# DRAM scratch of the attention operands in another axis order, and head outputs stored through another DMA queue

## The chip, the cores and the metric

The kernel runs on one core of a Trainium2 chip. The metric is the device time of one execution in microseconds (us). The kernel before takes 3268.81 us, the median of three runs (3268.14 to 3269.44).

## The reference

The program computes two layers of a transformer-like backbone on 512 latent and 256 context tokens (768 together) of width 1024. Each layer is a half-weight SwiGLU FFN, a token mixer and a second half-weight FFN, all with modulation, pre- and post-norm. The mixer of layer 0, which most of the change is about, is differential attention with 8 heads; each head has two score maps (m = 0, 1) over 64 features and one value matrix of 128 columns. Cut to what matters:

```python
q, k, v = split(h @ w_qkv)            # q, k: (n, 8 heads, 2 maps, 64); v: (n, 8, 128)
q_l, k_l = apply_rope(q_l), apply_rope(k_l)            # latent tokens only
s = einsum('bqhmd,bkhmd->bhmqk', q, k) * 64 ** -0.5
p = softmax(s, axis=-1)
a = p[:, :, 0] - lam * p[:, :, 1]
o = einsum('bhqk,bkhe->bqhe', a, v)
y = (rmsnorm(o, subln) * (1 - lam_init)) @ w_o
```

Context queries attend to context keys alone. The mixer of layer 1 is a bidirectional gated linear recurrence with 8 heads, whose normed and gated head outputs also go through an output projection.

## The kernel before

**Exact parts.** TensorE works on float32 numbers split in a high and a low part, hi + lo, each exact in its one-pass format (`split`, L187 on ScalarE and L188 on VectorE). A product is three matmuls: high times high, high times low, low times high.

**Attention by head pairs.** Layer 0's attention runs over four pairs of heads, p = 0 to 3. In a stage, TensorE projects the queries and then the keys of pair p (`proj`, L574) and its values (L1146), and between these matmuls it steps through the attention of pair p - 1 (`attn`); a `Ticker` deals out the steps in proportion to the TensorE work recorded. The projected q or k is rotated on GpSimd (`rotate`, L1120 to L1122), split into the tile `qkhl`, and stored to a DRAM scratch `st_d[p, w]` in one DMA of 128 partitions (`stored`, L1111). `qkhl` holds on its partitions (head and map j = 0 to 3, index i = 0 to 31) and along them (part v, rotation half a, token).

**Stacked operands.** The scores want the features of one head and map on 64 partitions, with both exact parts stacked to 128. `load_stack` (L896 to L914) reads the scratch back into such a tile `stk` (128 partitions, 5 columns of 768 tokens), one tile per head, in nine DMAs on the SP queue, all at L904: one of 128 rows and eight of 64 rows, each row 768 x 4 bytes. The scratch has the axes (v, a, j, i, token), so that the 64 rows of one part and one j are two runs of 32 rows that lie apart in DRAM. The stack of a pair's first head is asked for right behind the store of the keys, that of the second at the beginning of `attn`. The scores (L950, L951) then read `stk`; their row maximum is taken on VectorE (L953), the exponential on ScalarE (L960), the difference of the two maps on VectorE (L973), and its transposes on TensorE (L988) are split into `aT` (L990, L995) for the product with the values (L1008).

**Head outputs.** `finish` norms a head's values (L1029 on GpSimd, L1033 on TensorE, L1036 on VectorE) and stores them to DRAM, `on_d`, by one DMA on the SP queue (L1039). Layer 1 does the same at L1349. The output projection loads them again through the same ring of three buffers (`raw`, L158) through which all weights come: first `on_d`, then its part of the weights `da_wo`, head after head. While the last pair's attention runs, TensorE does the output projection of the first five heads (L653); the last three are left for `mixer_tail`.

**What sets the order.** Each engine runs its instructions in the order in which they were recorded. All loads and the stores named here are issued by SP one after the other, so that a DMA that waits holds back those behind it. A load into a `raw` buffer waits until the buffer's last user, a `split`, is done on VectorE (L188).

Of the kernel before, what the change touches and what calls it, by code (L numbers as in the profile page):

```python
# [23 lines left out]
NLAT = 512  # L24
# [16 lines left out]
def kernel(  # L41
# [56 lines left out]
    def ps_gv(shape):  # L98
# [6 lines left out]
        (p, w): dram.tile([2, 2, 4, 32, NTOK], F32, name=f"st_d{p}{w}") for p in range(NPAIR) for w in "qk"  # L105
# [24 lines left out]
    class Jobs:  # L130
        """Weight stream: loads run ahead of their use in the order of use."""
# [39 lines left out]
        def look(self, key, ahead):  # L171
            """Split up to the `ahead`-th unit after job key."""
            j = bisect.bisect_right(self.units, self.pos[key]) + ahead - 1
            self.upto(self.units[min(j, len(self.units) - 1)] + 1)

        def need(self, key, ahead=0):
            """The result of job key; the next `ahead` units are split beforehand too."""
            self.upto(self.pos[key] + 1)
            if ahead:
                self.look(key, ahead)  # L180
            return self.res.pop(key)
# [3 lines left out]
    def split(dst_hi, dst_lo, src):  # L185
        """src = dst_hi + dst_lo, both exact in the tensor engine's one-pass format."""
        nc.scalar.copy(out=dst_hi, in_=src)  # L187
        nc.vector.tensor_tensor(out=dst_lo, in0=src, in1=dst_hi.bitcast(F32), op=ALU.subtract)  # L188
# [21 lines left out]
    class Mods:  # L210
        """Modulation vectors: silu(c) w_mod + b_mod.  At the start, when the tensor engine is idle, on it, one
        contraction chunk per step; later the vector engine multiplies and adds up the contraction chunks, half of
        the columns at a time, and the tensor engine only sums over the partitions."""
# [11 lines left out]
        def start(self, parts, rings, wide=None):  # L225
            """wide: silu(c) padded to 32 columns, for the tensor engine."""
# [30 lines left out]
        def run(self):  # L257
            """On the tensor engine: one contraction chunk of one part per step."""
# [16 lines left out]
        def chunks(self):  # L275
            """On the vector engine: two contraction chunks of half of the columns per step."""
# [28 lines left out]
        def total(self, acc, l, part, h, nm):  # L305
            """Sums over the partitions."""
# [49 lines left out]
        def gains(self, g, si):  # L356
            """Post-norm gains times gates, as rows."""
# [6 lines left out]
        def pace(self, slots):  # L364
            """The vector engine's share of one of `slots` remaining places."""
# [6 lines left out]
        def due(self):  # L372
            """What is due on the tensor engine."""
# [29 lines left out]
    class Ticker:  # L403
        """Steps a generator of interleaved work in proportion to the tensor-engine time emitted."""
# [8 lines left out]
        def later(self, delay, fn):  # L413
            """fn after `delay` more of tensor-engine time."""
# [21 lines left out]
    class Events:  # L436
        """Calls at given places of the interleaved work."""
# [10 lines left out]
    class Boundary:  # L448
        """Post-norm, residual and the next pre-norm of one sub-layer, one token tile at a time."""
# [35 lines left out]
        def tail(self, emit_tile, extra={}):  # L485
            """emit_tile over the tiles; the norm stages of the tiles before it come at places of their own in each."""
# [38 lines left out]
        def advance(self, n):  # L525
            """The first n units of the feature-major modulated input of the next sub-layer, in two exact parts;
            a unit is two feature chunks of a block of 256 tokens."""
# [25 lines left out]
        def stream(self, mm):  # L553
            """mm(b, ks) over token blocks and pairs of feature chunks, behind the transposes."""
# [16 lines left out]
    def mm_k(ps_ap, w, mv, k, nk=KC):  # L571
        """One contraction chunk: the three products of the two exact parts of each side."""
# [5 lines left out]
    def proj(w, hT, pt, a, b, tick=None):  # L578
        """pt[:, :b-a] = w^T hT[.., a:b] over all of the contraction."""
# [27 lines left out]
    def add_o(l, tag, wsrc):  # L607
        """Heads below TAIL pass through the unit ring while the mixer's last heads are still computed."""
# [34 lines left out]
    def out_tile(t, aT, wos, y, firstg, tick=None, small=False):  # L643
        """Partial output projection of token tile t, added into y."""
# [27 lines left out]
    def ffn(l, i, fp, xt, B0, nt, nxt, mods, last=False, spill=False):  # L672
        """In- and out-projections in groups of d_ff chunks; returns the boundary to the next sub-layer."""
# [99 lines left out]
    with ExitStack() as st:  # L773
# [10 lines left out]
        # modulation vectors of the first pre-norm, through slots that the first FFN needs later  # L784
# [19 lines left out]
        # q of the first head pair, token block by token block as they become ready  # L804
# [51 lines left out]
    with ExitStack() as st:  # L856
# [23 lines left out]
        # lower bounds of the recurrence: softmax over depth, cumulative, less the first  # L880
# [15 lines left out]
        def load_stack(p, hh):  # L896
            """Scores' operands of one head: both exact parts stacked along the contraction.
            0, 1: queries of m = 0 (high, low) and m = 1 (low, high); 2, 3: the high part of the keys twice;
            4: the low part of the keys of both m."""
# [3 lines left out]
            def ld(p0, n, c, src):  # L903
                nc.sync.dma_start(out=st_[p0:p0 + n, c].bitcast(F32), in_=src)  # L904

            j = 2 * hh
            ld(0, 128, 0, q[:, :, j].rearrange("v a i t -> (v a) i t"))
            for m in range(2):
                for dup in range(2):
                    ld(64 * dup, 64, 2 + m, k[0, :, j + m])  # L910
                ld(64 * m, 64, 4, k[1, :, j + m])
            for v in range(2):
                ld(64 - 64 * v, 64, 1, q[v, :, j + 1])
# [14 lines left out]
        def attn(p, vh):  # L928
            """Attention of the two heads of pair p; yields between tensor-engine steps."""
# [36 lines left out]
            def combine(hh, t):  # L966
                """p0 - lam (s0 / s1) p1: s0 times the difference of the two softmaxes."""
# [33 lines left out]
            def av(hh, b):  # L1001
                """Values of one block of 256 queries."""
# [12 lines left out]
            def finish(hh):  # L1015
                """Norm of a head over its 128 values, gain, and store; the values are s0 times those of the softmax."""
# [22 lines left out]
                nc.sync.dma_start(out=on_d[0][2 * p + hh], in_=of)  # L1039
# [30 lines left out]
        def need_spread(key, ahead):  # L1070
            """As J.need, the units after it split while this one is used."""
# [14 lines left out]
        for p in range(NPAIR):  # L1086
            T.every = 45.5 / 42
            for wi, w in enumerate("qk"):
# [20 lines left out]
                def stored(ab_t=ab_t, hl=hl, w=w, p=p):  # L1109
                    split(hl[:, 0, :, NLAT:], hl[:, 1, :, NLAT:], ab_t[:, :, NLAT:])  # L1110
                    nc.sync.dma_start(out=st_d[p, w].rearrange("v a j i t -> (j i) (v a) t"),  # L1111
                                      in_=hl.rearrange("p v a t -> p (v a) t").bitcast(F32))
# [3 lines left out]
                def rotate(ab, ab_t=ab_t):  # L1116
                    """(A C - B S, A S + B C)"""
# [50 lines left out]
    def mixer_tail(l, tag, si, nt, nxt, fp, xp, outs):  # L1168
        """Last heads of the output projection and the boundary to the next FFN."""
# [18 lines left out]
    with ExitStack() as st:  # L1188
# [7 lines left out]
        # values of the first head pair, token block by token block  # L1196
# [15 lines left out]
    y_st = ExitStack()  # L1212
    with ExitStack() as st:
# [6 lines left out]
        def blk(ap, L):  # L1220
            """(blocks of 2L, halves, L) view of a token axis."""
            return ap.rearrange("p (n two l) -> p n two l", two=2, l=L)

        def scan(h, F, Kt, qv, gs, v2):
            """Both directions of head h.  F: decays; Kt: keys, then keys times the decays to the end of their
            block; qv: queries; Qt: queries times the decays from the start of their block; gs: silu(gate)."""
# [20 lines left out]
            def muls(lev):  # L1247
                """Queries and keys times the decays over the other half of the blocks of this level."""
# [238 lines left out]
```

## Time and profile before

| | |
|---|---|
| median of three runs | 3268.81 us |
| span of the profiled execution | 3260.0 us (no other time of that execution is given; the median is 8.8 us above it) |
| TensorE matmul busy | 3049.1 us (94%), 17,122 matmuls |
| VectorE, ScalarE, GpSimd busy | 1717.6, 962.2, 177.9 us |
| DMA moved | 321.76 MB, mean 99 GB/s |
| chain that ended last | TensorE 82%, DMA 4%, ScalarE 4%, VectorE 4%, SP's issue 3% |
| layer 0's attention in the span | from about 640 to 1210 us |

TensorE is busy nearly all the time, so what counts is where it is not, and what it was waiting for; a busy share of another engine says little by itself. A wait is put down to what came last. The column PEclk of the tables by stretch is the granted clock of TensorE as a share of full speed: 1.00 is 2.4 GHz, 0.50 is 1.2 GHz. The column "DMA share" is the mean busy share of the 16 DMA engines.

### The profile page before, as it was taken

What the parts mean: (1) busy time and instruction counts of PE and PEld (TensorE: products, weight loads), DVE (VectorE), ACT (ScalarE), POOL (GpSimd) and SP (SyncE); (2) the same over time, 40 slices, a digit from 0 to 9 for tenths busy, and PEclk for the clock granted to TensorE, in tenths of its full rate; (3) what the DMA queues carried; (4) which work ended last, traced back from release to release, by engine and by line L of the source; (5) the groups of instructions that cost most, each with busy time, mean ns of one, the idle gap of its engine ahead of it and who ended that gap; (6) DMA issues with size and microseconds to landing.
All of it is one profiled execution on the core that took longest, in us unless ns stands there. A gap on an engine that the chain in (4) does not pass through costs nothing.

```text
span 3260.0 us, 41074 instructions
## 1 busy us (share of the span) xinstructions
PE 3049.1 (94%) x17122; PEld 2577.9 (79%) x17122; DVE 1717.6 (53%) x2393; ACT 962.2 (30%) x1597; POOL 177.9 (5%) x219
## 2 busy tenths in 40 slices
PE   7999999967968589999999999999999999889998
PEld 5888888856757378888888888888889889678887
DVE  4556555634635367454444755444465666663344
ACT  4111111523424235111112411111263434442222
POOL 0000000311101001000000100000010000010000
PEclk9999999988989699999999999999999999999999
DMA  5333333222222232333322333333221111242221
GB/s 216 121 111 126 119 118 103 107 90 94 80 86 83 78 110 102 100 98 104 103 84 78 104 104 126 115 115 113 89 77 56 49 63 49 84 146 80 98 99 70
DMA packets 109066, 321.76 MB, mean 99 GB/s; under 512 B 10224, under 2 KB 10704, under 8 KB 108880
## 3 DMA queue, kind: packets, MB, share of 16 engines
q1 hardware_dynamic: 105232, 306.50, 27.8%
q0 software_dynamic: 1920, 6.34, 0.6%
q10 hardware_dynamic: 1728, 6.29, 0.5%
q8 instruction: 135, 2.21, 0.3%
q14 instruction: 51, 0.42, 0.0%
HBM read 292.83 MB, written 26.26 MB: 98 GB/s over the span
## 4 chain that ended last, share of the span: by engine, by line
PE 82%; DMA 4%; ACT 4%; DVE 4%; SPq 3%; issue 3%; POOL 1%; ACTq 0%; DVEq 0%; POOLq 0%
PE mm L574 41%; PE mm L653 20%; PE tp L574 9%; SPq L904 3%; PE tp L1370 2%; PE mm L1280 1%; PE tp L653 1%; PE mm L950 1%; PE gv L1008 1%; ACT tmp L395 1%; ACT tmp L545 1%; PE mm L951 1%; DMA mw<-in_w_mod_dram 1%; DMA stk<-st_d2q 1%; DMA stk<-st_d1q 1%
## 5 line engine op out<-in xcount | busy, mean ns | idle before, releaser
L574 PE MATMUL mm<-hT,hl 128*128 128x256 f32 (+1 forms) x7728 | 1407.6, 341 | 8.3 <-DVE hT L550 3.2
L574 PEld LDWEIGHTS mm<-hT,hl 128*128 128x128 f32 x7728 | 1199.3, 188 | 208.4 <-DVE hT L550 7.1
L653 PE MATMUL mm<-wo,a 128*128 128x512 f32 x2886 | 664.9, 390 | 0.5 <-DVE wo L188 0.5
L653 PEld LDWEIGHTS mm<-wo,a 128*128 128x128 f32 x2886 | 538.6, 188 | 115.4 <-DVE y L668 2.8
L670 DVE TENSOR_TENSOR y<-y,mm 128x1024 f32<-128x1024 f32 x163 | 199.0, 1221 | 500.0 <-PE mm L653 500.0
L188 DVE TENSOR_TENSOR hl<-raw,hl 128x1024 fp32r<-128x1024 f32 x250 | 306.8, 1238 | 173.2 <-ACT hl L187 173.1
L574 PE MATMUL tp<-hT,hl 128*128 128x512 f32 (+1 forms) x1824 | 381.8, 360 | 7.9 <-DVE aT L995 7.2
L574 PEld LDWEIGHTS tp<-hT,hl 128*128 128x128 f32 x1824 | 291.8, 192 | 53.8 <-DVE aT L995 9.3
L292 DVE SCALAR_TENSOR_TENSOR acc<-mw,cs,acc 128x512 f32<-128x512 f32 x392 | 271.5, 746 | 2.3 <-DMA mw<-in_w_mod_dram 0.7
L187 ACT CAST hl<-raw 128x1024 fp32r<-128x1024 f32 x250 | 258.2, 1046 | 47.2 <-DMA raw<-in_da_wo_dram 23.4
L187 ACT CAST a<-tmp 128x768 fp32r<-128x768 f32 (+1 forms) x88 | 68.8, 781 | 664.0 <-DVE tmp L747 664.0
L187 ACT CAST wo<-raw 128x1024 fp32r<-128x1024 f32 x94 | 98.1, 1045 | 462.6 <-PE mm L653 457.6
L731 ACT ACTIVATE tmp<-mm 128x768 f32<-128x768 f32 (+1 forms) x88 | 66.8, 759 | 406.7 <-PE mm L574 405.5
L747 DVE TENSOR_TENSOR tmp<-tmp,mm 128x768 f32<-128x768 f32 (+1 forms) x88 | 78.0, 886 | 201.1 <-PE mm L574 199.0
L950 PE MATMUL mm<-stk 128*128 128x512 f32 (+1 forms) x128 | 65.5, 511 | 97.6 <-DMA stk<-st_d3q 19.8
L953 DVE TENSOR_REDUCE nm<-mm 128x1 f32<-128x768 f32 (+1 forms) x96 | 73.3, 776 | 146.4 <-PE mm L951 143.6
L653 PE MATMUL tp<-hl,hT 128*128 128x512 f32 x300 | 92.0, 442 | 38.4 <-DVE aT L995 28.5
L950 PEld LDWEIGHTS mm<-stk 128*128 128x128 f32 (+1 forms) x128 | 25.4, 199 | 126.7 <-issue 112.0
L188 DVE TENSOR_TENSOR a<-tmp,a 128x768 fp32r<-128x768 f32 (+1 forms) x88 | 78.5, 892 | 74.6 <-ACT a L187 74.6
L188 DVE TENSOR_TENSOR wo<-raw,wo 128x1024 fp32r<-128x1024 f32 x94 | 114.8, 1223 | 5.5 <-ACT wo L187 5.5
L960 ACT ACTIVATE pt<-mm,nm 128x768 f32<-128x768 f32 (+1 forms) x96 | 72.7, 768 | 121.6 <-DVE nm L953 121.6
L653 PEld LDWEIGHTS tp<-hl,hT 128*128 128x128 f32 x300 | 57.6, 207 | 53.5 <-DVE aT L995 31.0
(187 smaller groups left out, 2448.8 us busy)
## 6 DMA issues: line engine op xcount, KB each, us to landing
raw<-in_w_in_dram SPq DMA_DIRECT2D x176, 512.0 KB
mw<-in_w_mod_dram SPq DMA_DIRECT2D x144, 512.0 KB
raw<-in_w_out_dram SPq DMA_DIRECT2D x88, 512.0 KB
raw<-in_hg_w_dram SPq DMA_DIRECT2D x32, 512.0 KB
raw<-in_da_qk_dram SPq DMA_DIRECT2D x16, 512.0 KB
gg<-gg_d POOLq DMA_DIRECT2D x12, 512.0 KB, 4.8
xp<-x_d SPq DMA_DIRECT2D x10, 512.0 KB
raw<-in_da_v_dram SPq DMA_DIRECT2D x8, 512.0 KB
```

Source lines behind the costliest of these rows:

```text
L187: nc.scalar.copy(out=dst_hi, in_=src)
L188: nc.vector.tensor_tensor(out=dst_lo, in0=src, in1=dst_hi.bitcast(F32), op=ALU.subtract)
L292: nc.vector.scalar_tensor_tensor(out=acc[:, m], in0=raw[:, kk], scalar=cs[:, k, m:m + 1], in1=acc[:, m], op0=ALU.mult, op1=ALU.add)
L574: nc.tensor.matmul(out=ps_ap, lhsT=w[a], rhs=mv[b], start=(k == 0 and i == 0), stop=(k == nk - 1 and i == 2))
L653: nc.tensor.matmul(out=po if small else po[:, hh * 512:(hh + 1) * 512], lhsT=aT[ci][:, u, t * P:(t + 1) * P], rhs=wos[ci][:, v, hh * 512:( ...
L670: nc.vector.tensor_tensor(out=dst, in0=dst, in1=src, op=ALU.add)
L731: nc.scalar.activation(out=sg[:, :width], in_=pg[:, :width], func=AF.Silu)
L747: nc.vector.tensor_tensor(out=sg[:, :width], in0=sg[:, :width], in1=pu[:, :width], op=ALU.mult)
L904: nc.sync.dma_start(out=st_[p0:p0 + n, c].bitcast(F32), in_=src)
L950: nc.tensor.matmul(out=sc[:, 0:NLAT], lhsT=lhs, rhs=rhs[:, 0:NLAT], start=(i == 0), stop=(i == 1))
L953: nc.vector.tensor_reduce(out=nm, in_=sc[:, :n], axis=AX.X, op=ALU.max, negate=True)
L960: nc.scalar.activation(out=pt[:, :n], in_=scs[m][:, :n], func=AF.Exp, bias=nms[m], accum_out=s0s[hh][:, t:t + 1] if m == 0 else s1)
```

## The change

The scratch `st_d` has the axes (j, v, a, i, token) in place of (v, a, j, i, token), so that the 64 rows of one part and one j lie one behind the other. The store of q or k is four DMAs of 32 partitions in place of one of 128. The stack of a head comes in ten loads of 64 consecutive rows, in place of one of 128 and eight of 64, and the operands of m = 0 come ahead of those of m = 1. The stores of head outputs, in both layers, are issued by GpSimd. The texts that describe functions are taken out, which changes no instruction but moves the line numbers: L904 becomes L905, L1111 L1116, L1039 L1043, L1349 L1354.

```diff
     st_d = {
-        (p, w): dram.tile([2, 2, 4, 32, NTOK], F32, name=f"st_d{p}{w}") for p in range(NPAIR) for w in "qk"
+        (p, w): dram.tile([4, 2, 2, 32, NTOK], F32, name=f"st_d{p}{w}") for p in range(NPAIR) for w in "qk"
     }
...
             q, k = st_d[p, "q"], st_d[p, "k"]
 
-            def ld(p0, n, c, src):
-                nc.sync.dma_start(out=st_[p0:p0 + n, c].bitcast(F32), in_=src)
+            def ld(half, c, src):
+
+                nc.sync.dma_start(out=st_[64 * half:64 * half + 64, c].bitcast(F32),
+                                  in_=src.rearrange("a i t -> (a i) t"))
 
             j = 2 * hh
-            ld(0, 128, 0, q[:, :, j].rearrange("v a i t -> (v a) i t"))
+            for v in range(2):
+                ld(v, 0, q[j, v])
             for m in range(2):
                 for dup in range(2):
-                    ld(64 * dup, 64, 2 + m, k[0, :, j + m])
-                ld(64 * m, 64, 4, k[1, :, j + m])
-            for v in range(2):
-                ld(64 - 64 * v, 64, 1, q[v, :, j + 1])
+                    ld(dup, 2 + m, k[j + m, 0])
+                ld(m, 4, k[j + m, 1])
+                if m == 0:
+                    for v in range(2):
+                        ld(1 - v, 1, q[j + 1, v])
             stk[p, hh] = st_
...
-                nc.sync.dma_start(out=on_d[0][2 * p + hh], in_=of)
+                nc.gpsimd.dma_start(out=on_d[0][2 * p + hh], in_=of)
...
-                    nc.sync.dma_start(out=st_d[p, w].rearrange("v a j i t -> (j i) (v a) t"),
-                                      in_=hl.rearrange("p v a t -> p (v a) t").bitcast(F32))
+                    for j in range(4):
+                        nc.sync.dma_start(out=st_d[p, w][j].rearrange("v a i t -> i (v a) t"),
+                                          in_=hl[32 * j:32 * j + 32].rearrange("p v a t -> p (v a) t").bitcast(F32))
...
-            nc.sync.dma_start(out=on_d[1][h][:, 0:NLAT], in_=of)
+            nc.gpsimd.dma_start(out=on_d[1][h][:, 0:NLAT], in_=of)
```

On SP, this is the order around the store of the keys of pair 2 in the kernel before (`st_d2k` is the scratch of pair 2's keys, `stk` a head's stack, `on_d_2` the output of head 2, `raw` a buffer of the weight stream):

```order
L1111 DMA st_d2k<-qkhl 128x4x768
L904 DMA stk<-st_d2q 128x1x768
L904 DMA stk<-st_d2k 64x1x768 x6
L904 DMA stk<-st_d2q 64x1x768 x2
L1039 DMA on_d_2_89<-of 128x768
L904 DMA stk<-st_d2q 128x1x768
L904 DMA stk<-st_d2k 64x1x768 x6
L904 DMA stk<-st_d2q 64x1x768 x2
L158 DMA raw<-in_da_v_dram 128x1024 x2
```

And this is the same place in the changed kernel:

```order
L1116 DMA st_d2k<-qkhl 32x4x768 x4
L905 DMA stk<-st_d2q 64x768 x2
L905 DMA stk<-st_d2k 64x768 x3
L905 DMA stk<-st_d2q 64x768 x2
L905 DMA stk<-st_d2k 64x768 x3
L905 DMA stk<-st_d2q 64x768 x2
L905 DMA stk<-st_d2k 64x768 x3
L905 DMA stk<-st_d2q 64x768 x2
L905 DMA stk<-st_d2k 64x768 x3
L158 DMA raw<-in_da_v_dram 128x1024 x2
```

The store of head 2's output has left SP; the two stacks follow each other, and one column of q (m = 1) has moved ahead of the second group of k.

On GpSimd, this is the order before around the norm factor `r` of the heads 0 and 1 and the first rotation of pair 2's q (`t`):

```order
L1029 TENSOR_TENSOR r_5768<-r_5768,halfc 128x6
L1029 TENSOR_TENSOR r_6174<-r_6174,halfc 128x6
L1120 TENSOR_TENSOR t_6515<-ab_t,CSt 128x512
L1121 TENSOR_TENSOR t_6516<-ab_t,CSt 128x512
L1122 TENSOR_TENSOR t_6515<-t_6515,t_6516 128x512
```

And this is that place in the changed kernel:

```order
L1033 TENSOR_TENSOR r_5779<-r_5779,halfc 128x6
L1043 DMA on_d_0_87<-of 128x768
L1033 TENSOR_TENSOR r_6189<-r_6189,halfc 128x6
L1043 DMA on_d_1_88<-of 128x768
L1125 TENSOR_TENSOR t_6531<-ab_t,CSt 128x512
L1126 TENSOR_TENSOR t_6532<-ab_t,CSt 128x512
L1127 TENSOR_TENSOR t_6531<-t_6531,t_6532 128x512
```

The stores of the heads 0 and 1 now stand on GpSimd, that of head 1 ahead of the rotation. The order on TensorE, VectorE and ScalarE is the same in both kernels.

## Rows read from the trace of the kernel before

**Rows 1.** TensorE's waits over the span: total us, times, longest us

```profile
PE tp L653 <- DVE aT L995: 28.5, 5, 25.9
```

**Rows 2.** Line 904: durations ns min/median/max; then who waited, us and times

```profile
L904 SPq DMA_DIRECT2D stk<-st_d1k x12: 484/3660/4187, 780.4 to 825.7; - x12
...
L904 SPq DMA_DIRECT2D stk<-st_d0q x6: 671/3698/3701, 659.2 to 715.6; - x6
...
  PE mm L950: 97.5, 11
```

**Rows 3.** Chain that ended last, 900 to 950 us: start, us, what

```profile
905.98 6.18 DMA st_d2k<-qkhl
...
928.73 19.64 DMA stk<-st_d2q
...
948.46 0.77 PE mm L950
```

**Rows 4.** Busy time by stretch; last columns PEclk, DMA share, GB/s

```profile
684.00:688.00 4.00, 0.00 (x0) 0.00 (x0) 0.00 (x0) 0.00 (x0) 0.00 (x0) 0.50 0.13 51
...
1188.00:1192.00 4.00, 4.00 (x28) 3.52 (x26) 1.20 (x3) 2.57 (x4) 0.00 (x0) 1.00 0.83 317
```

**Rows 5.** SP and TensorE in order of time, where the pairs' scores begin

```profile
658.60 0.38 SPq L1111 DMA_DIRECT2D st_d0k<-qkhl  x1
...
774.17 0.38 SPq L1111 DMA_DIRECT2D st_d1k<-qkhl  x1
...
1029.91 0.37 SPq L1111 DMA_DIRECT2D st_d3k<-qkhl  x1
...
676.77 0.77 PE L950 MATMUL mm<-stk 128*128 128x512 f32 x1 [4.97 <-DMA stk<-st_d0k]
...
793.33 0.47 PE L950 MATMUL mm<-stk 128*128 128x512 f32 x1 [0.28 <-DMA stk<-st_d1k]
...
924.39 0.47 PE L950 MATMUL mm<-stk 128*128 128x512 f32 x1 [3.62 <-DMA stk<-st_d2k]
...
1047.82 0.50 PE L653 MATMUL tp<-hl,hT 128*128 128x512 f32 x1 [3.00 <-ACT hl L187]
1048.39 0.60 PE L950 MATMUL mm<-stk 128*128 128x512 f32 x1
```

**Rows 6.** ScalarE, SP and VectorE in order of time, last pair

```profile
1115.08 1.04 ACT L187 CAST hl<-raw 128x1024 fp32r<-128x1024 f32 x1 [23.43 <-DMA raw<-in_da_wo_dram]
...
1096.64 3.61 SPq L158 DMA_DIRECT2D raw<-in_da_wo_dram  x1
...
1079.80 0.96 DVE L188 TENSOR_TENSOR hT<-raw,hT 128x768 fp32r<-128x768 f32 x1
```

**Rows 7.** Busy time of nine stretches behind TensorE's waits, the longest and their sum

```profile
1073.00:1089.00 16.00, 16.00 (x46) 11.74 (x47) 7.72 (x12) 7.21 (x14) 1.99 (x1) 0.50 0.13 50
...
sum 57.00, PE 44.00 PEld 31.74 DVE 22.80 ACT 15.99 POOL 4.00; mean PE 4.89 PEld 3.53 DVE 2.53 ACT 1.78 POOL 0.44
```

**Rows 8.** GpSimd's loads of gains (count, busy us, mean ns; then us to landing)

```profile
L386 POOL DMA_DIRECT2D gg<-gg_d x12 | 6.8, 567 | 685.9 <-DMA raw<-in_w_in_dram 460.6 <-DVE acc L292 225.2
...
DMA to landing us min/median/max: 3.8/4.8/5.4
```

**Rows 9.** SP and VectorE in order of time, end of attention; GpSimd and ScalarE, a rotation

```profile
1199.46 0.33 SPq L1039 DMA_DIRECT2D on_d<-of  x1
...
1203.29 3.49 DVE L188 TENSOR_TENSOR wo<-raw,wo 128x1024 fp32r<-128x1024 f32 x3
...
831.71 2.01 POOL L1120 TENSOR_TENSOR t<-ab_t,CSt 128x512 f32<-128x512 f32 x1 [5.63 <-ACT ab_t L1103]
...
849.83 0.47 DVE L1036 SCALAR_TENSOR_TENSOR of<-of,sub,gv 128x256 f32<-128x256 f32 x1
...
857.88 0.63 ACT L187 CAST qkhl<-t 128x512 fp32r<-128x512 f32 x1
```

**Rows 10.** TensorE's waits from 1700 us to the end, the longest

```profile
PE tp L541 <- ACT y L483: 7.9, 4, 4.4
```

## Prediction

> **What bounds the kernel now.** I read TensorE's waits first, since TensorE is busy 94% of the span. Nearly all that it waits for is in layer 0's attention: 97.5 us in 11 pieces of the scores (L950) for the stacked operands [rows 2], and 25.9 us in one piece of the output projection (L653) that is put down to VectorE [rows 1]. From 1700 us on no wait for a DMA is among TensorE's; the longest there, 7.9 us, is for ScalarE [rows 10]. So the change can gain in the attention and hardly elsewhere.
>
> The chain of waits says how a stage begins: the keys' store takes 6.2 us, then SP issues loads, and the last of these, q of m = 1, is what the scores wait 19.6 us for [rows 3]. The loads are slow one by one. A load of 64 rows (196,608 B) holds SP for 3.70 us and one of 128 rows (393,216 B) for 3.70 us as well [rows 2]. While they run the 16 DMA engines are busy to a share of 0.13, that is 2 of 16, at 51 GB/s; with all engines in use 317 GB/s go through at a share of 0.83 [rows 4]. A 64-row load has two runs of rows and keeps 2 engines busy; the 128-row load has four runs and moves twice as much in the same time, 4 engines. The loads are short of engines, not of memory.
>
> The 25.9 us are the same thing at second hand: ScalarE idled 23.4 us for a weight load issued at 1096.64, behind the last of the second stack's slow loads; its buffer had been free since the split of 1079.80 plus 0.96 [rows 6].
>
> **The change, part by part.** *Loads of 64 consecutive rows.* The first run of such a load is all of its 64 rows, so I expect it on all 16 engines. No row shows that shape, so I bound it: from above by the rate of all engines, 317 GB/s, from below by half of it. At 317 GB/s a pair's store of 1,572,864 B takes 5.0 us, and the 6.18 us of rows 3 leave 1.2 us for its beginning and end. Ten loads, 1,966,080 B, take 6.2 us. SP issues a load in 0.49 us where nothing holds it back [rows 2], ten in 5, so issuing is no limit. The loads need not wait for the whole store, only for their own j, and follow it through the same queue: 5.0 + 6.2 + 1.2 = 12.4 us from the keys' store to the last operand.
>
> When does TensorE want them? It reached the first scores at 676.77 - 4.97 = 671.8, 793.33 - 0.28 = 793.05, 924.39 - 3.62 = 920.8 and 1048.39 us; the keys' stores were issued at 658.60, 774.17, 905.98 and 1029.91 [rows 3, 5]. That leaves 13.2, 18.9, 14.8 and 18.5 us, and 1 us more for m = 1. So 12.4 us are in time in all four stages, by 1.8 us in the tightest. Of the 97.5 us I let 2 stay (none at the best, 10 where the loads run at some three quarters of the rate): **95.5 us** gained. The second stack has several tiles of attention in hand and is no concern.
>
> *The weight load behind them.* With the second stack off SP in some 6 us, the load of 1096.64 can go as soon as its buffer is free, but it then shares the engines with that stack, and TensorE now arrives sooner too, at full clock. Between nothing and 10 us of the wait may stay; I take 5: **20.9 us** of 25.9.
>
> *The clock.* After a wait the granted clock of TensorE is 0.50, or 1.2 GHz, and comes back only after some us of work. Nine stretches behind the waits named hold 44.0 us of busy time at 0.50 to 0.55; the longest is 16 us at 1073 [rows 7]. At 2.4 GHz that work takes half, so 22 us are at stake. But ahead of the last pair's scores TensorE also idles 3.00 us for ScalarE [rows 5], which the change leaves, and the clock was down right behind it; up to 11 us may stay, I take 6: **16 us**.
>
> *Stores of q and k in four.* 24 more issues of 0.38 us on SP [rows 5], beside work of TensorE: nothing. If four stores of 32 partitions are slower than one, that comes under the half rate below.
>
> *Head outputs through GpSimd.* A DMA holds GpSimd for 0.57 us and lands after 4.8 us, for 512 KB [rows 8]; 16 of them make 9 us on an engine busy 5% of the span. Two places could be late. At the end of the attention the last head's store went out at 1199.46; through GpSimd it lands by 1199.5 + 0.6 + 4.8 = 1204.9. Its load is the third into buffers that VectorE frees by 1203.29 + 3.49 = 1206.8 [rows 9]: 1.9 us of cover. And head 1's store now stands ahead of pair 2's rotation. GpSimd began that at 831.71, but the store waits for VectorE until 849.83 + 0.47 = 850.3. The three operations, 1.3 us each, then end at about 854.8, and ScalarE takes the result at 857.88 [rows 9]: 3 us of cover. Both cost nothing; without their cover it would be 1 to 3 us apiece. Behind the store wait only GpSimd's own next operations. Layer 1's stores free SP from waits that TensorE does not feel [rows 10]: no gain, and 0 to 1 us of loss at its end.
>
> *Sum.* 95.5 + 20.9 + 16 = 132.4 us. The profiled execution's span of 3260.0 becomes 3127.6; the median of the runs is 8.8 us above that span, so **3136 us**. At the best 97.5 + 25.9 + 22 = 145.4, or 3123; with the larger remainders 87.5 + 15.9 + 11 = 114.4, or 3154. That is the forecast's own range.
>
> **The rivals.** *Half rate.* A tile of 64 partitions may take its data no faster than half of a tile of 128, however many engines carry it; every row of 16 engines above is of 128 partitions, so none speaks against it. At 158 GB/s stores take 9.9 us and ten loads 12.4, with the 1.2 us 23.5 us to the last operand, against 14.2, 19.9, 15.8 and 19.5 us in hand with the 1 us for m = 1: waits of 9.3, 3.6, 7.7 and 4.0 us, 24.6 in all. With the larger remainders at the weight load and the clock: 72.9 + 15.9 + 11 = 99.8 us gained, **3169 us**. The Trainium skill speaks for this rival (SBUF — State Buffer, section "Door 1: The DMA port swizzle"): the partitions 0 to 63 reach only 8 of the 16 ports on the DMA side, no more than 32 partitions do, and it measured 196 GB/s for them. With that figure stores and loads would take an estimated 8.0 and 10.0 us, the waits would come to 8.4 us, and the time to 3153. No run here shows it yet.
>
> *The weight load stays late.* If something else holds SP at that place (a buffer freed late, a load of a head's output that waits for GpSimd's store), the 25.9 us stay, and 2 us of clock behind them: **3159 us**. For it speaks that the load's buffer frees only while TensorE works on the first scores; against it that in the trace that was 16 us before the issue [rows 6].
>
> *The loads do not spread.* If 64 consecutive rows still go to few engines, each takes the 3.70 us of before, and a stack is ten loads, not nine: 3.7 us more in each of four stages and once more at the weight load, 18.5 us, **3287 us**, slower. It decides from 33.3 / 10 = 3.3 us a load on. Against it: four runs were carried by 4 engines and two by 2, so the count follows the slowest axis [rows 2, 4].
>
> **How the numbers follow.** I give the forecast 0.56, the half rate 0.25, the late weight load 0.12, the loads that do not spread 0.04; 0.03 is for gains and losses not thought of. The range runs from 3122, the best sum, to 3172, just past the half rate: it leaves out the loads that do not spread and the tails. 0.2% of the time, 6.5 us, is about what a measurement of this kernel can tell from no change. All cases but one are faster by far more: faster 0.95, same 0.01, slower 0.04.
>
> **What would show it.** In the changed profile, loads at L905 that hold SP for 0.5 to 0.7 us and a DMA share well above 0.13 show the first step right; 1.0 to 1.3 us apiece at a share near 0.5 show the half rate; 3.7 us, no spread. TensorE's waits at the scores for `stk` should be 0 to 10 us together, the piece at L653 under 10 us, and the clock 1.00 through the beginnings of the first three stages. On GpSimd, rotations that begin later but no wait of ScalarE or TensorE for them. The forecast is wrong if the waits for `stk` come back as waits for something else of the same size, such as the weights' splits, or if TensorE finds its operands and the span still does not shrink by 110 us.

## The result, and the profile after

The changed kernel takes 3146.7 us, 0.963 of the time before (95% interval 0.9615 to 0.9640); measured again beside the experiments it took 3146.7 us once more, a ratio of 0.9635 (0.9618 to 0.9653). The forecast was 3136 us, with its own range up to 3154.

The page of the changed kernel begins so (busy us, share of the span, instructions):

```profile
span 3147.3 us, 41132 instructions
...
PE 3046.8 (97%) x17122; PEld 2577.1 (82%) x17122; DVE 1716.1 (55%) x2393; ACT 961.3 (31%) x1597; POOL 185.8 (6%) x235
```

TensorE's busy time is nearly what it was (3049.1 us before): of the 112.7 us that the span lost, 110.4 were idle. Its waits in layer 0's attention, 640 to 1215 us (total us, times, longest us):

```profile
PE mm L653 <- ACT oa L187: 5.9, 1, 5.9
PE mm L954 <- DMA stk<-st_d0k: 5.6, 2, 2.9
...
PE tp L653 <- DVE aT L999: 5.0, 5, 2.3
PE mm L954 <- DMA stk<-st_d2k: 3.8, 3, 2.9
...
PE tp L653 <- ACT hl L187: 3.0, 1, 3.0
```

The 97.5 us for the stacks [rows 2] are 5.6 + 3.8 = 9.4 us, and only in the stages of pairs 0 and 2, the two with the least time in hand. The 28.5 us of L653 put down to VectorE [rows 1] are 5.0. A load of 64 rows holds SP for 0.6 us where it was 3.7 [rows 2] (ns min/median/max, first and last start):

```profile
L905 SPq DMA_DIRECT2D stk<-st_d1k x12: 554/595/1210, 760.6 to 772.1; - x12
...
L905 SPq DMA_DIRECT2D stk<-st_d0q x8: 594/595/2164, 666.0 to 678.8; - x8
```

Three stretches of the changed kernel (last columns PEclk, DMA share, GB/s):

```profile
672.00:674.00 2.00, 0.00 (x0) 0.00 (x0) 0.00 (x0) 0.00 (x0) 0.00 (x0) 1.00 1.02 250
...
678.00:682.00 4.00, 3.33 (x11) 2.49 (x12) 0.96 (x1) 0.38 (x1) 0.00 (x0) 0.50 1.04 240
...
886.00:890.00 4.00, 4.00 (x11) 2.64 (x10) 0.10 (x1) 0.00 (x0) 1.16 (x1) 0.50 0.10 40
```

While TensorE waits (672 to 674) all 16 engines are busy, a share of 1.02 against 0.13 [rows 4], but they move 250 GB/s and not the 317 that the forecast took. And behind the waits, now of 3 us, the clock is still 0.50.

That last is a loss in the busy time. I count it as the sum, over stretches of 1 us, of TensorE's busy time times (1 - granted clock), and call it the clock loss below: 38.3 us before (27.3 in the attention, 8.2 from 1700 us on), 38.0 after (23.0 and 11.2). So the account of the 112.7 us is: 97.5 - 9.4 = 88.1 from the stacks, 28.5 - 5.0 = 23.5 behind the weight load, 0.3 from the clock; together 111.9. This compares one execution with one. In e6 below, which runs the same instructions up to an added tail, the clock loss ahead of that tail was 32.4 us (18.3 in the attention), so the clock's part is known to some 6 us only.

### The profile page after: what moved, and what is told of

Same layout as the page of the kernel before. It is cut to its first block, busy times and chain, and to the rows that moved or that the text cites. A ratio compares the mean times of both kernels' runs of the same rounds, so it can differ in the third digit from the quotient of the medians.

```text
span 3147.3 us, 41132 instructions
## 1 busy us (share of the span) xinstructions
PE 3046.8 (97%) x17122; PEld 2577.1 (82%) x17122; DVE 1716.1 (55%) x2393; ACT 961.3 (31%) x1597; POOL 185.8 (6%) x235
## 4 chain that ended last, share of the span: by engine, by line
PE 84%; DVE 4%; ACT 4%; issue 3%; DMA 2%; POOL 1%; SPq 0%; ACTq 0%; DVEq 0%; POOLq 0%
PE mm L574 43%; PE mm L653 21%; PE tp L574 8%; PE tp L1375 2%; PE mm L954 1%; PE gv L1012 1%; PE tp L653 1%; PE tp L1151 1%; PE mm L1285 1%; PE mm L955 1%; ACT tmp L395 1%; PE tp L992 1%; ACT tmp L545 1%; DMA mw<-in_w_mod_dram 1%; DVE hl L188 1%
## 5 line engine op out<-in xcount | busy, mean ns | idle before, releaser
L653 PE MATMUL mm<-wo,a 128*128 128x512 f32 x2886 | 664.9, 390 | 0.5 <-DVE wo L188 0.5
L653 PEld LDWEIGHTS mm<-wo,a 128*128 128x128 f32 x2886 | 538.5, 188 | 115.4 <-DVE y L668 2.6
L670 DVE TENSOR_TENSOR y<-y,mm 128x1024 f32<-128x1024 f32 x163 | 199.0, 1221 | 500.3 <-PE mm L653 500.3
L653 PE MATMUL tp<-hl,hT 128*128 128x512 f32 x300 | 89.5, 432 | 16.5 <-DVE hl L188 5.1
L653 PEld LDWEIGHTS tp<-hl,hT 128*128 128x128 f32 x300 | 55.7, 201 | 31.8 <-DVE aT L999 7.5
L994 ACT CAST aT<-tp 128x384 fp32r<-128x384 f32 (+1 forms) x80 | 33.7, 461 | 144.5 <-PE tp L992 144.4
L1151 PE MATMUL tp<-hl,hT 128*128 128x256 f32 x576 | 75.1, 284 | 0.1
```

The source lines that it names most:

```text
L653: nc.tensor.matmul(out=po if small else po[:, hh * 512:(hh + 1) * 512], lhsT=aT[ci][:, u, t * P:(t + 1) * P], rhs=wos[ci][:, v, hh * 512:( ...
L670: nc.vector.tensor_tensor(out=dst, in0=dst, in1=src, op=ALU.add)
L1151: nc.tensor.matmul(out=pv[:, tt], lhsT=hT[:, k, a, t * P:(t + 1) * P], rhs=wk[:, b], start=(k == 0 and i_ == 0), stop=(k == KC - 1 and i_ ...
```

## The experiments

Ratios are to the kernel before, with 95% intervals; each run has its own runs of before on the same chip. Clock loss is that of the profiled execution, over the span, in the attention and from 1700 us on.

| run | us | ratio | waits for stk | clock loss |
|---|---|---|---|---|
| changed kernel again (a_again) | 3146.7 | 0.9635 (0.9618 to 0.9653) | 7.2 | 38.3, 24.0, 11.6 |
| e1 layout only | 3139.3 | 0.9614 (0.9601 to 0.9626) | 7.5 | 30.1, 20.4, 8.3 |
| e2 GpSimd only | 3270.4 | 1.0013 (1.0004 to 1.0022) | 97 | 42.1, 31.0, 10.5 |
| e3 one store | 3135.0 | 0.9604 (0.9591 to 0.9616) | 1.2 | 28.0, 13.8, 11.4 |
| e5 one store, SP | 3132.1 | 0.9587 (0.9573 to 0.9601) | 1.8 | 31.4, 18.8, 9.5 |
| e9 one store, layer 1 on SP | 3128.7 | 0.9577 (0.9563 to 0.9591) | 1.6 | 27.4, 16.7, 9.3 |
| e10 late keys | 3140.0 | 0.9611 (0.9595 to 0.9627) | 6.1 | 29.3, 17.3, 9.6 |
| e11 layer 0 on SP | 3144.3 | 0.9624 (0.9611 to 0.9637) | 6.4 | 34.7, 18.4, 13.5 |
| e12 layer 1 on SP | 3139.7 | 0.9617 (0.9604 to 0.9630) | 10.2 | 37.2, 23.1, 10.0 |
| e14 scores first | 3127.7 | 0.9576 (0.9563 to 0.9589) | 2.0 | 24.8, 11.3, 10.6 |
| e15 old layout | 3133.0 | 0.9589 (0.9576 to 0.9602) | 0.9 | 27.4, 13.4, 10.9 |

**The changed kernel again**, nothing edited.

> The changed kernel once more, beside the three others of this group. All theories: the same time as in its first measurement, 3147 us to within 0.3%, with about 9.4 us of TensorE's waits for stk and no clock gained.

The same time, 7.2 us of waits for stk (9.4 were expected), and no clock gained. Its runs spread from 3138 to 3153 us, so differences of 3 us between kernels cannot be told from none.

**The layout alone (e1), and GpSimd alone in the kernel before (e2).**

```diff
-                nc.gpsimd.dma_start(out=on_d[0][2 * p + hh], in_=of)
+                nc.sync.dma_start(out=on_d[0][2 * p + hh], in_=of)
...
-            nc.gpsimd.dma_start(out=on_d[1][h][:, 0:NLAT], in_=of)
+            nc.sync.dma_start(out=on_d[1][h][:, 0:NLAT], in_=of)
```

(e1; e2 is the opposite edit in the kernel before.)

> The changed layout, stores and loads, with the head outputs' stores back on SP. Theory (the layout does it all): the time of the changed kernel, 3147 us, within 5 us; TensorE waits for stk 9 to 12 us, and at the output projection (L653) for VectorE at most 5 us. Rival (taking the stores off SP is what lets the weight load go in time): the store of head 1 waits on SP for VectorE in front of loads, up to 24 us come back at L653, and the time is 3160 to 3172 us.

> The kernel before with only the head outputs' stores moved to GpSimd. Theory (the store's place is worth nothing): the time of the kernel before within 5 us; TensorE's 97.5 us for stk and about 26 us at L653 stay. Rival (SP was held by these stores): the waits for stk or at L653 fall by 10 to 25 us, 3243 to 3258 us. If the layout alone (the other run) loses what this one gains, the two parts add up; if both lose nothing, the stores' place is idle.

The new scratch with its loads and stores makes the whole gain, and the stores through GpSimd cost: e1 is 7 us faster than the changed kernel, with intervals that just overlap (up to 0.9626, from 0.9618), and e2 is 4 us slower than before, which its interval tells from none. So e1's own theory held in the cause but not in its numbers: it put the time at 3147 us within 5 and the waits for stk at 9 to 12 us, and they are 3139.3 and 7.5. The rival of a freed SP is out: in e2 the wait behind the weight load stays 25.0 us long (25.9 in [rows 1]), and in e1, with the stores back on SP, it does not return.

**One store of 128 partitions (e3).** The four stores were a step that the forecast had priced at nothing. In the changed kernel, this is q's store of pair 0 on SP, then the cast that waits for it on ScalarE, then the store of the keys on SP:

```profile
645.28 4.13 SPq L1116 DMA_DIRECT2D st_d0q<-qkhl  x4
...
655.71 0.62 ACT L187 CAST qkhl<-t 128x512 fp32r<-128x512 f32 x1 [5.24 <-DMA st_d0q<-qkhl]
...
661.80 4.11 SPq L1116 DMA_DIRECT2D st_d0k<-qkhl  x4
```

In the kernel before, the same cast, and a stretch of the store's transfer:

```profile
651.18 0.63 ACT L187 CAST qkhl<-t 128x512 fp32r<-128x512 f32 x1 [0.65 <-DMA st_d0q<-qkhl]
...
647.00:649.00 2.00, 2.00 (x19) 2.00 (x18) 1.28 (x1) 0.72 (x2) 1.65 (x2) 1.00 1.03 401
```

`qkhl` is a single buffer: the split of k waits until q's store has read it. Four stores take 655.71 - 645.28 = 10.4 us to let it go, one takes 651.18 - 645.35 = 5.8 us. So the keys' store goes out at 661.80, not 658.60 [rows 5].

```diff
-        (p, w): dram.tile([4, 2, 2, 32, NTOK], F32, name=f"st_d{p}{w}") for p in range(NPAIR) for w in "qk"
+        (p, w): dram.tile([4, 32, 2, 2, NTOK], F32, name=f"st_d{p}{w}") for p in range(NPAIR) for w in "qk"
...
-                ld(v, 0, q[j, v])
+                ld(v, 0, q[j, :, v])
...
-                    for j in range(4):
-                        nc.sync.dma_start(out=st_d[p, w][j].rearrange("v a i t -> i (v a) t"),
-                                          in_=hl[32 * j:32 * j + 32].rearrange("p v a t -> p (v a) t").bitcast(F32))
+                    nc.sync.dma_start(out=st_d[p, w].rearrange("j i v a t -> (j i) (v a) t"),
+                                      in_=hl.rearrange("p v a t -> p (v a) t").bitcast(F32))
```

> Scratch with the axes (j, i, v, a, token): q and k are stored by one DMA of 128 partitions again, and the ten loads of 64 rows stay, their rows now every fourth or second row of DRAM. Theory (four stores of 32 partitions cost 10.4 us where one costs 5.8, and since qkhl is a single buffer the keys' split waits for the queries' store): the cast of k in stage 0 is released about 6 us after the store of q, not 10.4; the keys' store goes out at about 658.6 and takes about 6 us; the waits for stk fall from 9.4 us to 0 to 3 us. If small waits cost the clock as much as long ones, 8 to 10 us of clock come back in stages 0 and 2: 3125 to 3137 us. Rival 1 (loads of rows that lie apart are slower than of consecutive ones, or go to fewer engines): waits for stk of 10 us or more, 3147 us or above. Rival 2 (the waits go, but the clock is lost to the other small waits, of VectorE and ScalarE): 3138 to 3142 us, with the clock still 0.50 at the heads of stages 0 and 2.

In this kernel the cast is released, and the keys are stored, at (ScalarE, SP), and the wait for stk that is left and a stretch of loads beside the scores are:

```profile
650.57 0.62 ACT L187 CAST qkhl<-t 128x512 fp32r<-128x512 f32 x1 [0.63 <-POOL t L1125]
...
658.02 0.33 SPq L1114 DMA_DIRECT2D st_d0k<-qkhl  x1
...
PE mm L953 <- DMA stk<-st_d0k: 1.2, 1, 1.2
...
869.00:871.00 2.00, 1.87 (x9) 1.26 (x8) 1.50 (x2) 1.03 (x3) 0.00 (x0) 1.00 1.07 246
```

The theory held: the keys go out at 658.02, 1.2 us of waits are left, the clock is 1.00 through the scores of pair 2 (0.50 from 878 to 894 in the changed kernel), and the attention's clock loss falls from 24.0 (the changed kernel again) to 13.8 us. The loads, of rows that lie apart, run at 246 GB/s, as fast as the 250 of consecutive ones.

**Transfers by themselves (e6).** Behind the end of the changed kernel, so that its time (3310.6 us, one run) says nothing:

```diff
+        for rep in range(2):
+            for i in range(10):
+                ld(64 * (i % 2), i // 2, src[i % 4, i // 4 % 2].rearrange("a i t -> (a i) t"))
+            done(big[:, :, 0:1], P)
...
+            for i in range(5):
+                ld(0, i, src[i % 4].rearrange("v a i t -> (v a i) t"), 128)
```

> The changed kernel with transfers by themselves added behind its end, seven groups, twice: ten loads of 64 consecutive rows to the two halves in turn; ten to partitions 0 to 63; five loads of 128 consecutive rows; the ten of the first group, the halves on two queues (SP and ScalarE); four loads of 64 rows in two runs apart, as before the change; one store of 128 partitions, then a load; four stores of 32 partitions, then a load. Theory (a tile of 64 partitions takes its data at some 0.6 of the rate of one of 128, whichever half and however the queues are shared): 225 to 260 GB/s in the first, second and fourth group, 350 to 400 in the third, at a DMA share near 1 in all four; the fifth 51 GB/s at a share of 0.13; the store about 6 us, the four stores about 10. Rival 1 (half rate by the partitions alone): 1.9 times as long for the first as for the third. Rival 2 (the halves together reach the full rate, and other traffic slowed the loads inside the kernel): the first takes as long as the third, the second twice as long. Rival 3 (the queue limits): the fourth is faster than the first.

The steady middle of each group, in the order of the expectation (stretch first, PEclk, DMA share and GB/s last; the third is of the first round, and from 3252 to 3257, in the second, that group moved 331 GB/s):

```profile
3229.00:3235.00 6.00, 0.00 (x0) 0.00 (x0) 0.00 (x0) 0.00 (x0) 0.00 (x0) 0.50 0.98 258
3240.00:3247.00 7.00, 0.00 (x0) 0.00 (x0) 0.00 (x0) 0.00 (x0) 0.00 (x0) 0.50 1.01 210
3170.00:3174.00 4.00, 0.00 (x0) 0.00 (x0) 0.00 (x0) 0.00 (x0) 0.00 (x0) 0.50 0.99 369
3261.00:3267.00 6.00, 0.00 (x0) 0.00 (x0) 0.00 (x0) 0.00 (x0) 0.00 (x0) 0.50 1.03 267
3273.00:3286.00 13.00, 0.00 (x0) 0.00 (x0) 0.00 (x0) 0.00 (x0) 0.00 (x0) 0.50 0.13 50
3288.00:3292.00 4.00, 0.00 (x0) 0.00 (x0) 0.00 (x0) 0.00 (x0) 0.00 (x0) 0.50 0.94 393
3297.00:3303.00 6.00, 0.00 (x0) 0.00 (x0) 0.00 (x0) 0.00 (x0) 0.00 (x0) 0.50 0.97 216
```

With every engine busy, 64 partitions in one half take 210 GB/s, the two halves in turn 258 (267 over two queues), 128 partitions 369; 32 partitions store 216, 128 store 393. So the share says how many engines carry a transfer and not how fast it goes. The expectation's "whichever half" fell: one half alone is below the 225 to 260 GB/s expected, and taking the halves in turn gives a quarter more. The load behind the one store goes out 5.1 us after it, that behind the four 8.7 us (6 and 10 were expected).

The Trainium skill (SBUF — State Buffer, "Door 1: The DMA port swizzle") gives 196 GB/s for 64 partitions, and 189 for 32; the 210 and 216 here lie 7% and 14% above. The same page's section "Can I just issue two DMAs to hit both halves?" measured only 6% for two halves at once; here it is 258 / 210, 23%, and the measurement decides.

**Whether the layout is needed (e15).** The scratch and the store as before the change; the loads take their rows with the index i outermost:

```diff
-                nc.sync.dma_start(out=st_[p0:p0 + n, c].bitcast(F32), in_=src)
+                nc.sync.dma_start(out=st_[64 * half:64 * half + 64, c].bitcast(F32),
+                                  in_=src.rearrange("a i t -> i a t"))
```

> The scratch as before the change (v, a, j, i, token), one store of 128 partitions, all stores of head outputs on SP; only the loads are read in another order: ten of 64 rows, in the order of the change, their rows taken as 32 groups of 2 (index i outermost, rotation half a inside) instead of 2 groups of 32, so that partition 2i + a of both operands holds the row (a, i). Theory (what decides is how many steps the outermost axis of a load has, 32 here and 2 before, not whether the 64 rows lie together): loads hold SP 0.5 to 0.6 us each, the DMA share beside the scores is near 1, the waits for stk are 0 to 3 us in all and the time is that of the same kernel with the axes (j, i, v, a, token), 3132 us, within 4 us. Rival (the rows have to lie near each other in DRAM): loads slower than 1 us each, waits for stk of 20 us or more, over 3155 us.

A group of its loads (ns min/median/max), its waits for stk, and a stretch beside them:

```profile
L905 SPq DMA_DIRECT2D stk<-st_d2k x12: 507/597/1102, 859.7 to 871.7; - x12
...
PE mm L954 <- DMA stk<-st_d0k: 0.9, 1, 0.9
...
672.00:676.00 4.00, 3.00 (x19) 2.20 (x18) 1.91 (x2) 1.50 (x3) 0.00 (x0) 1.00 1.05 240
```

3133.0 us, the 3132.1 of e5 within their intervals: with one store and SP's stores of head outputs the old layout is as good as a new one, and better than the changed kernel. What spread the loads is 32 steps on the outermost axis in place of 2; that the 64 rows lie together did nothing. No run isolates the order of the loads (m = 0 ahead of m = 1).

**Where GpSimd's stores cost (e5, e9, e11, e12).** Each is the edit of e1, or its half for one layer, in e3 (e5: both layers, e9: layer 1) or in the changed kernel (e11: layer 0, e12: layer 1).

> The one store of 128 partitions and the loads of 64 rows lying apart, as in the run before with that layout (3135.0 us, span 3131.0), and the head outputs' stores back on SP in both layers. Theory (a store through GpSimd starts earlier and takes its 1.2 us of all DMA engines from the stack's loads; where these no longer are waited for, that costs nothing): in layer 0 no change, waits for stk of 0 to 2 us. In the recurrence, half-clock work falls from 11 us to the 8 us that both kernels with SP's stores show: 3130 to 3135 us. Rival (a store through GpSimd costs wherever it is): 5 to 8 us less, 3127 to 3130 us. Second rival (SP is held by these stores, and a weight load is late): over 3137 us.

> As the one above, but only the stores of layer 1 back on SP; those of layer 0 stay with GpSimd. If the recurrence is what the stores through GpSimd cost in this layout, its time is that of the one above (3130 to 3135 us) and below the 3135 us of the layout with all stores on GpSimd; if layer 0, it is that of the latter. Half-clock work from 1700 us on: 8 us if layer 1's stores decide it, 11 us if not.

> The changed kernel with layer 0's head outputs stored through SP again and layer 1's through GpSimd. The changed kernel takes 3146.7 us, that with all of these stores on SP 3139.3 us. If GpSimd's store beside the stack's loads of pair 2 is what costs (a wait of 2.5 to 2.9 us against 1.7, and the half clock behind it), this comes to 3139 to 3143 us, with 11 us of half-clock loss from 1700 us on. If layer 1 alone decides, 3146 us.

> The changed kernel with layer 1's head outputs stored through SP again and layer 0's through GpSimd. If layer 1's stores through GpSimd cost 2 to 3 us of clock in the recurrence (11 us of half-clock loss from 1700 us on in four kernels with them, 8 to 10 in five without), this comes to 3142 to 3145 us with 8 to 10 us of that loss; if they cost nothing, 3146 us. If the two parts add up, the gain of this run and of the one before make the 7 us together.

The traces show a cost in both layers. In layer 0, the store of head 2, which stood on SP behind the first stack of pair 2 before, now goes out as soon as it is ready, among the stack loads of pair 2 (GpSimd of the changed kernel; then its queue's packets, MB and share of 16 engines, 858 to 878 us):

```profile
862.75 0.62 POOL L1043 DMA_DIRECT2D on_d<-of  x1 [7.16 <-DVE of L1040]
...
q0 software_dynamic: 80, 0.39, 6.1%
```

It takes 6.1% of 20 us, 1.2 us of all engines, ahead of the operands of m = 1. These are then 2.46 to 2.87 us late in the four profiles of this layout with layer 0's stores on GpSimd (the changed kernel twice, e6, e12), and behind that wait the clock loss is 8.5, 8.4, 1.7 and 8.5 us. In e1 and e11, where SP issues the store behind the first stack, the wait is a single one of 1.69 and 1.87 us, and the clock stays at 1.00 behind it (e1):

```profile
877.50 0.47 PE L954 MATMUL mm<-stk 128*128 128x512 f32 x1 [1.69 <-DMA stk<-st_d2k]
...
878.00:882.00 4.00, 4.00 (x24) 3.33 (x24) 2.20 (x4) 1.93 (x3) 0.00 (x0) 1.00 1.06 267
```

In layer 1, a wait of TensorE's of 1.6 to 2.1 us at the end of the output projection, for VectorE's sum `y` (L670), is there in all six profiles with GpSimd's stores; in the eight with SP's it is at most 0.5 us. Here is that wait in the changed kernel again, with GpSimd's last norm factor and its two loads of gains `gg` (512 KB each) behind it, and then the same two in e1:

```profile
PE tp L653 <- DVE y L670: 1.8, 1, 1.8
...
2715.70 1.03 POOL L1345 TENSOR_TENSOR r<-r,halfc 128x4 f32<-128x4 f32 x1 [40.70 <-DVE r L1344]
2720.42 1.08 POOL L386 DMA_DIRECT2D gg<-gg_d  x2
...
2713.71 1.01 POOL L1345 TENSOR_TENSOR r<-r,halfc 128x4 f32<-128x4 f32 x1 [44.31 <-DVE r L1344]
2714.67 1.14 POOL L386 DMA_DIRECT2D gg<-gg_d  x2
```

With the last head's store on GpSimd, these loads stand behind it and go out 4.72 us after the norm factor instead of 0.96, about when SP issues the last two loads of weights. ScalarE's cast of the first of these waits 6.1 to 6.7 us for its load in the six profiles and 4.3 to 5.1 in the eight, and VectorE's sum comes behind that weight's split. No run moves the loads of gains alone, so this chain is read from the traces and not tested. The clock loss from 1700 us on is 10.5 to 13.5 us (mean 11.6) in the six and 8.2 to 10.9 (mean 9.6) in the eight.

By time, even the two layers together are hardly told from none in this layout (0.9614 against 0.9635). e11 and e12 lie between, but neither at the time that its theory gave (3139 to 3143 and 3142 to 3145 us expected, 3144.3 and 3139.7 measured; the profiled execution of e12, at 3146.7 us, is the slowest of its four), and e3, e5 and e9 do not order as either theory has it. How much falls to which layer stays open.

**A late store of the keys (e10), in e5.**

```diff
+                    for _ in range(2 if (p, w) == (2, "k") else 1):
```

> As the first, with one thing added: the store of pair 2's keys is made twice, so that the first stack's loads of that stage follow about 6 us later. In that stage the operands came at the moment they were wanted, so TensorE now waits about 5 to 6 us for stk, in one place. Theory (a wait of some 3 us or more at the scores costs about 8 us of clock behind it, whatever its length): 13 to 15 us slower than the first. Rival (the clock's loss was of other origin): slower by the wait alone, 5 to 6 us. Second rival (something else hides it): under 3 us.

The last wait of three for stk (4.5 us in all) that this makes in pair 2's stage:

```profile
874.07 0.76 PE L953 MATMUL mm<-stk 128*128 128x512 f32 x1 [2.94 <-DMA stk<-st_d2k]
```

The clock is down from 874 to 881 only, a loss of 3.4 us; the kernel is 7.9 us slower than e5 by the runs, 4.3 by the spans. Waits for stk grew by 6.1 - 1.8 = 4.3 us, so by the spans the wait alone, the first rival, accounts for it. My theory of a fixed 8 us behind each such wait fell.

**The scores ahead of the output projection (e14), in e9.**

```diff
+        next(outs)
+        next(T.gen)
```

(with a `yield` in `o_groups` behind the first fetch)

> The kernel with one store of 128 partitions, loads of 64 rows apart, and layer 1's stores on SP (3128.7 us, span 3127.6), in which TensorE still waits 3.00 us for ScalarE at the first matmul of the output projection (L653), with 8.4 us of half-clock loss behind it in that stage. Here the first scores of the last pair are recorded ahead of that projection, so that TensorE has them to do while ScalarE casts; the prediction put up to 11 us of clock down to this wait. Theory (that wait is what brings the clock down there): the 3.0 us and 6 to 8 us of clock go, 3118 to 3121 us. Rival (the clock is down for another reason at the head of a stage, such as the many short scores with slack between them): only the 3 us of wait go, 3125 to 3127 us, and the half-clock stretch of some 16 us stays. Second rival: the scores then wait for their operands 1 to 3 us, and nothing is gained.

Two waits at L653 in its place, and a stretch of that stage:

```profile
964.84 0.49 PE L653 MATMUL tp<-hl,hT 128*128 128x512 f32 x1 [0.88 <-ACT hl L187]
...
966.11 0.73 PE L653 MATMUL tp<-hl,hT 128*128 128x512 f32 x2 [0.77 <-DVE hl L188]
...
971.00:975.00 4.00, 4.00 (x13) 2.50 (x12) 1.85 (x2) 0.06 (x1) 0.84 (x1) 0.50 1.05 246
```

The 3.00 us became 0.88 + 0.77, and the clock still fell, with 6.5 us of loss from 966 to 981 (8.4 in e9). 3127.7 us is e9's 3128.7 within the intervals. The first rival held in the clock; its 3 us of time are too few to tell.

## Why the prediction was right, and where its terms were off

**Stack waits, 95.5 us forecast, 88.1 measured.** Right in mechanism: the loads went from 2 engines to 16. Two sizes were off. The rate: "at 317 GB/s" came from loads of 128 partitions, and tiles of 64 take some 250. That 64 partitions take less is what the half rate rival said, though its 158 GB/s was too low; 250 is close to the three quarters of the rate for which the forecast let 10 us of waits stay, and 9.4 stayed. And "stores of q and k in four: nothing" was wrong: they are slow, and q's holds up k's. From the keys' store to the last operands it takes 678.67 - 661.80 = 16.9 us in pair 0's stage and 877.41 - 857.60 = 19.8 in pair 2's, where the forecast had 12.4 and that rival 23.5:

```profile
678.67 0.77 PE L954 MATMUL mm<-stk 128*128 128x512 f32 x1 [2.95 <-DMA stk<-st_d0k]
...
857.60 4.12 SPq L1116 DMA_DIRECT2D st_d2k<-qkhl  x4
...
877.41 0.47 PE L954 MATMUL mm<-stk 128*128 128x512 f32 x1 [2.87 <-DMA stk<-st_d2k]
```

The error stayed small because two stages had 18.5 us and more in hand and showed no wait at all, as was forecast. e3, with one store again and the loads at 246 GB/s, has 1.2 us of waits left, within the 2 that the forecast let stay.

**Weight load, 20.9 forecast, 23.5 measured.** Right; the 5 us allowed for traffic were not needed.

**Clock, 16 forecast, 0.3 measured.** The step that failed. I took the clock's loss to go with the length of the waits: nine stretches behind the waits named, so most of it gone with them. But waits of 3 us were left at the same places, and the clock fell behind them as well: 8.5 us of loss behind the 2.87 us above, 8.1 at the 3.00 us that the change leaves, of which I had let 6 stay. It came back where a stage had no wait left (pair 1, and pair 2 in e3), and in e1 and e11 also behind the 1.69 and 1.87 us left in pair 2's stage. What decides the size is not settled: behind waits of 2.5 to 2.9 us at the scores of pair 2 the losses were 8.5, 8.4 and 8.5 us, but 1.7 in e6 and 3.4 in e10; behind the 2.95 us in pair 0's stage it was 2.3; and e14 lost 6.5 behind 0.88 and 0.77.

**Head outputs through GpSimd, nothing forecast, some 4 to 7 us lost.** I looked at who waits for GpSimd's compute, and nobody does; what I left out is the transfers. One that goes out earlier (head 2's store) takes the engines from another that is waited for, and GpSimd's own next operations, which I dismissed, are at the end of layer 1 loads that go out later, among loads of weights. For that end I had allowed 0 to 1 us; TensorE waits 1.6 to 2.1.

**The 8.8 us from span to median.** The profiled executions of the changed kernel and of the experiments take 1.7 to 1.9 us more than their spans, so some 7 of the 8.8 mean that the profiled execution of the kernel before was a fast one. By spans the forecast was 132.4 us against 112.7, by medians against 3268.81 - 3146.7 = 122.1. That 3136 came within 11 us and not 20 is owed to which executions were profiled, and is luck.

**Rivals and readings.** The rivals of a late weight load and of loads that do not spread are out by the rows above. Two readings were loose, and neither enters the sum: of TensorE's 210.9 us idle before, the waits named are 123, not nearly all; and the 7.9 us of [rows 10] are four waits, the longest 4.4.

The lowest times are those of e9 and e14, 3128.7 and 3127.7 us, some 18 us below the changed kernel.

## What to carry to other kernels

Read a slow transfer by two numbers, the share (how many engines) and the rate at full share (how many partitions), and price a new shape by a row with the same partitions, not by the best rate on the page. Before changing a layout, look at the outermost axis of the load: another order of the same rows may do. Count time at half clock as given back only where a run shows it: a shorter wait at the same place may cost as much clock as a long one. Ask of each transfer that is freed whose engines it takes, and what now stands behind it on its new queue.

## What the hardware showed that was not expected

Stores of 32 partitions run at 216 GB/s with all 16 engines busy, against 393 for 128. Loads of 64 rows that lie apart, two of every four (e3) or from two distant runs in turn (e15), run as fast (240 to 246 GB/s) as of consecutive ones. The clock stays at 0.50 for 16 us behind a wait of 2.87 us while TensorE is busy throughout; in another execution of the same instructions (e6) it is at 0.50 for some 3 us behind a wait of 2.70.
